# Six modulation vectors of a DiT-like network summed on TensorE instead of VectorE

## The chip, the cores and the metric

One NeuronCore of one Trainium2 chip runs the whole network as one program. The metric is the device time of one execution in microseconds (us); lower is better. TensorE (PE) multiplies, VectorE (DVE) and ScalarE (ACT) work on rows and evacuate results, SyncE (SP) issues nearly all loads.

## The reference, cut to what matters

An fp32 network over 256 tokens of width 1024: two layers of a mixer and a feed-forward part (the second of these a mixture of eight experts, two for each token), then two layers of attention and a feed-forward part. Each of the eight sublayers is modulated by a scale, a shift and a gate, which come from one conditioning vector c and a weight matrix:

```python
def modulation(c, w, b):
    m = jnp.einsum("bd,de->be", jax.nn.silu(c), w) + b
    shift, scale, gate = jnp.split(m, 3, axis=-1)
    return shift[:, None], scale[:, None], gate[:, None]
```

So there are 24 modulation vectors of 1024 numbers, each the product of silu(c) with a matrix of 1024x1024, that is of 4 MB of weights. The sublayer's input is xn * (1 + scale) + shift, its result is multiplied by the gate and added to x.

## The kernel before

The program goes through stages 1 to 8 (mixer, FFN, mixer, experts, attention, FFN, attention, FFN). Stage 4 has two parts: the route (norm, router, choice of experts, expert input) and the experts. Weights come in chunks of 1 MB (128 partitions x 2048) into the pool raw, are split by ScalarE (L159) and VectorE (L160) into a rounded part hi and a rest lo, and each product takes three matmuls (mm3, L178 to L180). Matmuls of plain fp32 go through mm (L183) and leave two records each in the trace; transposes go through tr (L187).

The modulation vectors are computed ahead of their use, named by (layer, sub, scale/shift/gate) with layers and subs from 0. A stage's plan lists those that it makes, and calls of fill spread their steps over the stage; one step is one chunk of 1 MB. There are two ways:

- mod_rows keeps a running sum macc of 128x1024 on VectorE: for each of eight rows of 128 weights macc += w * c (L318 for the first, L320 for the others), with c one number for each partition. At the end TensorE sums over the partitions: for a gate two matmuls with a matrix of ones, 128x512; for a scale or shift (in stages other than 2 and 6) eight matmuls that take 128 columns of macc as the weight and one column of ones, and L353 adds the bias.
- mod_gate_pe, before for the gate (0,0) alone, lets TensorE do the whole sum: sixteen matmuls of 128x512 that take c, spread over 128 columns, as the weight and the chunk as the moving side, and two with the bias.

The order on each engine is set by a scheduler that builds the program: code emitted earlier has priority, and fill is put back by LAG; within one engine the instructions then run strictly in the order given. SP is such a queue too: a load that waits for its buffer holds back all loads behind it. The pool raw has four buffers.

```python
        LAG = {1: 100, 3: 100, 4: 30, 5: 30}
        FILL = {1: (4, 1, 1, 3, 1, 2), 2: (3, 2, 2), 3: (1, 1, 1, 1, 0, 0), 6: (2, 3), 8: (1, 0)}
```

Names used below: raw is a loaded chunk, h a stage's modulated input, x and xn the residual stream and its norm, P attention probabilities, ysum the sum of the experts' results; pp, pa, pj, sa, sb, sd are pools of TensorE's results. L1071 to L1113 choose the experts, L1152 and behind it builds the experts' input.

Of the kernel before, what the change touches and what calls it, by code (L numbers as in the profile page):

```python
# [15 lines left out]
ALU = mybir.AluOpType  # L16
# [3 lines left out]
D = 1024  # L20
KD = 8
# [46 lines left out]
class _Net:  # L68
# [186 lines left out]
    def fill(self, n):  # L255

        with self.behind(), self.tc.high_priority(offset=-self.lag) if self.lag else nullcontext():
            for _ in range(n):
                if not self.modq:
                    return  # L260
                key = self.modq[0]
                if key in self.gates_pe:
                    self.mod_gate_pe(key)
                else:
                    self.mod_rows(key)
                self.modpos += 2
                if self.modpos == KD:
                    self.modpos = 0
                    self.modq.pop(0)
                    self.mods[key] = self.mod_done(key)  # L270
# [8 lines left out]
    def mod_gate_pe(self, key):  # L279

        nc = self.nc
        w, b, j, c0 = self.mod_src(key)
        if self.modpos == 0:
            self.modacc = self.tl("gate", [128, D])
            nc.gpsimd.dma_start(out=self.modacc[0:1, :], in_=b[j * D:(j + 1) * D].unsqueeze(0))
        g = self.modacc
        h, k0 = self.modpos // 4, self.modpos % 4 * 2
        hs = slice(h * 512, (h + 1) * 512)
        if k0 == 0:
            self.modps = self.ps(pool="pa")  # L290
            self.mm(self.modps, self.ones[0:1, :], g[0:1, hs], True, False)
        wv = w.rearrange("(k p) n -> p k n", p=128)
        v = self.raw(wv[:, k0:k0 + 4, j * D + h * 512:j * D + (h + 1) * 512])
        for i in range(4):
            c = self.csil[:, c0 + k0 + i:c0 + k0 + i + 1]
            self.mm(self.modps, c.to_broadcast([128, 128]), v[:, i], False, k0 + i == KD - 1)
        if k0 == 4:
            self.plus(key, g[:, hs], self.modps)

    def mod_rows(self, key):  # L300

# [19 lines left out]

    def mod_done(self, key):

        if key in self.gates_pe:
            return self.modacc
        l, s, name = key
        j, acc = self.mod_src(key)[2], self.modacc
        if name == "gate":
            g = self.tl("gate", [128, D])
            for h in range(2):  # L330
                hs = slice(h * 512, (h + 1) * 512)
                p = self.ps(pool=self.mps)
                self.mm(p, self.ones, acc[:, hs])
                self.plus(key, g[:, hs], p)
            return g
        c = self.tl("col", [128, KD])
        if self.step in (2, 6):

            sums = self.sc([128, KD])
            for k in range(0, KD, 4):  # L340
                p = self.ps((128, 4, 128), pool=self.mps)
                for q in range(4):
                    self.tr(p[:, q], acc[:, (k + q) * 128:(k + q + 1) * 128])
                for q in range(4):
                    self.nc.scalar.activation(p[:, q], p[:, q], ACT.Copy, accum_out=sums[:, k + q:k + q + 1])
        else:
            p = self.ps(pool=self.mps)
            for k in range(KD):
                self.mm(p[:, k:k + 1], acc[:, k * 128:(k + 1) * 128], self.ones[:, 0:1])
            sums = p[:, 0:KD]  # L350
        q = ((l * 2 + s) * 3 + j) * KD if l < 2 else ((l - 2) * 6 + j) * KD
        bc = (self.col3 if l < 2 else self.col4)[:, q:q + KD]
        self.nc.vector.scalar_tensor_tensor(c, sums, 1.0 if name == "scale" else 0.0, bc, ALU.add, ALU.add)  # L353
        return c
# [1146 lines left out]
    def run(self):  # L1501
        a, nc = self.a, self.nc
        FFN = dict(f=2, s2=10, sh=12, pp=4, pa=4)
        MIX = dict(sh=3, s1=2, w=4, g=3, kvl=1, cx=2, ct=4, cv=6, dc=3, cb=2, ys=2, ml=3, P=3, pj=2, sd=3, pa=3)
        ROUTE = dict(sh=4, s1=2, s2=4)
        MOE = dict(pp=2, ya=2, pa=4)
        EXP = dict(xe=1, s1=4, s2=6, s4=2, rawx=2)
        ATT = dict(sh=5, s1=2, qk=2, sq=3, v=2, qkT=6, on=3, P=5, y=6, pp=2, pj=2, sa=2, sb=2)
        SIZES = {1: MIX, 2: FFN, 3: MIX, 4: MOE, 5: ATT, 6: dict(FFN, f=4), 7: ATT, 8: FFN}

        SC, SH, GA = "scale", "shift", "gate"
        plan = {
            0: [(0, 0, SC), (0, 0, SH)],
            1: [(0, 0, GA), (0, 1, SC), (0, 1, SH)],
            2: [(0, 1, GA), (1, 0, SC), (1, 0, SH), (1, 0, GA), (1, 1, SC), (1, 1, SH)],
            3: [(1, 1, GA)],
            4: [(2, 0, SC), (2, 0, SH), (2, 0, GA)],
            5: [(2, 1, SC), (2, 1, SH)],
            6: [(2, 1, GA), (3, 0, SC), (3, 0, SH), (3, 0, GA), (3, 1, SC), (3, 1, SH)],
            8: [(3, 1, GA)],  # L1520
        }
        self.gates_pe = {(0, 0, GA)}
        LAG = {1: 100, 3: 100, 4: 30, 5: 30}
        FILL = {1: (4, 1, 1, 3, 1, 2), 2: (3, 2, 2), 3: (1, 1, 1, 1, 0, 0), 6: (2, 3), 8: (1, 0)}
        self.mods, self.modq, self.modpos = {}, [], 0
        with self.phase(sh=12, s1=1, s2=3, pp=4, pa=4):
            setup = self.setup()
            next(setup)
            self.mod_start(plan[0])
            x = self.load_x(a["x"])  # L1530
            xn = x = self.layer_norm(x)
            self.fill(KD * KD)
            for _ in setup:
                pass
            g, b = self.c1("ln0_g", 0), self.c1("ln0_b", 0)
            self.later = [lambda x=x: self.affine(x, a["ln0_g"], a["ln0_b"])]
        for s in range(1, 9):
            l, i = (s - 1) // 2, (s - 1) % 2
            self.step = s
            one = s < 5  # L1540
            if s == 2:
                self.later.append(self.rope_setup)
            with self.phase(**SIZES[s]):
                if one:
                    A, B = self.ab(l, i, g, b)
                else:
                    A, B = self.ab(l, i, self.c1("norm_ffn_2" if i else "norm_mix_2", l - 2))
                if s == 4:
                    self.bar = None
                    with self.phase(**ROUTE):  # L1550
                        self.mod_start(plan[4], LAG[4])
                        self.fill(KD * KD)
                        hf = self.make_hf(xn, A, B)
                        st = self.route(xn, hf)
                    with self.phase(**EXP):
                        order = self.granules()
                        ready = [self.raw(src) for src in order[:5]]
                        ready = [self.split(v) for v in ready[:2]] + ready[2:] + [self.raw(order[5])]
                        self.moe_over(st, A, B)
                        ysum = st[4]  # L1560
                        self.experts(0, *st[:4], A, B, ysum, order, True, ready)
                    get = lambda t, hh: ysum[t][hh]
                else:
                    h = self.make_h(xn, A, B)
                    self.mod_start(plan.get(s, []), LAG.get(s, 0))
                    if i == 0:
                        get = self.mixer(l, h, FILL[s]) if one else self.attn2(l - 2, h)
                    elif one:
                        get = self.ffn(h, a["ffn_w1"][0], a["ffn_w3"][0], a["ffn_w2"][0], FILL[s])
                    else:  # L1570
                        get = self.ffn(h, a["w_gate_2"][l - 2], a["w_up_2"][l - 2], a["w_down_2"][l - 2], FILL[s])
                rows = (a["post_ln_g"][l, i], a["post_ln_b"][l, i]) if one else None
                if s == 4:
                    x, xn = self.resid_rms(get, x, self.mod(l, i, "gate"), self.two_rows(*rows))
                else:
                    x, xn = self.resid(get, x, self.mod(l, i, "gate"), one, s < 8)
                if s < 4:
                    g, b = self.c1("post_ln_g", s - 1), self.c1("post_ln_b", s - 1)
                    x = xn
                    self.later.append(lambda x=x, r=rows: self.affine(x, *r))  # L1580
# [35 lines left out]
```

## Time and profile before

| | before |
|---|---|
| median of 3 runs (lowest to highest) | 2068.33 us (2067.39 to 2068.36) |
| profiled execution: its time, its span | 2068.1 us, 2066.0 us |
| TensorE busy | 1926.2 us, 93% |
| VectorE busy | 1643.8 us, 80% |
| ScalarE busy | 1208.2 us, 58% |
| mean granted clock of TensorE | 0.972 of full speed |

The span is the profiled part of one execution, and the time of that execution is 2.1 us longer. Busy time of TensorE counts matmuls; it can be busy at two clocks, 1.2 and 2.4 GHz, which the profile gives as granted clocks of 0.50 and 1.00.

### The profile page before, as it was taken

What the parts mean: (1) busy time and instruction counts of PE and PEld (TensorE: products, weight loads), DVE (VectorE), ACT (ScalarE), POOL (GpSimd) and SP (SyncE); (2) the same over time, 40 slices, a digit from 0 to 9 for tenths busy, and PEclk for the clock granted to TensorE, in tenths of its full rate; (3) what the DMA queues carried; (4) which work ended last, traced back from release to release, by engine and by line L of the source; (5) the groups of instructions that cost most, each with busy time, mean ns of one, the idle gap of its engine ahead of it and who ended that gap; (6) DMA issues with size and microseconds to landing.
All of it is one profiled execution on the core that took longest, in us unless ns stands there. A gap on an engine that the chain in (4) does not pass through costs nothing.

```text
span 2066.0 us, 29939 instructions
## 1 busy us (share of the span) xinstructions
PE 1926.2 (93%) x11481; PEld 1660.4 (80%) x11481; DVE 1643.8 (80%) x2412; ACT 1208.2 (58%) x1817; POOL 50.2 (2%) x100
## 2 busy tenths in 40 slices
PE   3998999898499999999999999969989999998999
PEld 3887999886378787878778888858869998978998
DVE  6888987898598888888888888889778887667554
ACT  3455445562488767767776777755554546555442
POOL 4000000100000000000000000000000000000000
PEclk9999999998699999999999999979999999999999
DMA  9576999665399999899999999958339995326662
GB/s 325 184 276 214 348 329 316 195 223 205 144 330 362 339 332 341 319 357 346 345 326 350 348 355 358 364 187 279 138 119 349 335 328 164 123 86 220 204 204 82
DMA packets 283238, 555.25 MB, mean 269 GB/s; under 512 B 10172, under 2 KB 137520, under 8 KB 283088
## 3 DMA queue, kind: packets, MB, share of 16 engines
q1 hardware_dynamic: 280000, 549.49, 75.1%
q0 software_dynamic: 2656, 3.20, 0.9%
q8 instruction: 91, 1.49, 0.3%
q10 hardware_dynamic: 432, 0.58, 0.1%
q14 instruction: 59, 0.48, 0.1%
HBM read 552.19 MB, written 1.05 MB: 268 GB/s over the span
## 4 chain that ended last, share of the span: by engine, by line
PE 63%; DVE 6%; ACT 2%; issue 2%; DMA 0%; ACTq 0%; DVEq 0%
PE pp L179 11%; PE pp L180 11%; PE pp L178 11%; PE pa L654 6%; PE ya L179 4%; PE ya L178 4%; PE ya L180 4%; PE pp L187 3%; DVE lo L160 2%; PE pj L178 2%; PE pj L179 1%; PE pj L180 1%; PE sa L183 1%; PE pp L183 1%; ACT hi L159 1%
## 5 line engine op out<-in xcount | busy, mean ns | idle before, releaser
L160 DVE TENSOR_TENSOR lo<-raw,hi 128x1024 fp32r<-128x1024 f32 x660 | 786.0, 1219 | 177.3 <-ACT hi L159 168.6
L159 ACT CAST hi<-raw 128x1024 fp32r<-128x1024 f32 x660 | 667.4, 1050 | 344.2 <-PE pp L179 141.8
L178 PE MATMUL pp<-h,hi 128*128 128x256 f32 x960 | 270.7, 282 | 0.0
L180 PE MATMUL pp<-h,lo 128*128 128x256 f32 x960 | 267.8, 279 | 0.0
L179 PE MATMUL pp<-h,hi 128*128 128x256 f32 x960 | 267.7, 279 | 0.0
L160 DVE TENSOR_TENSOR lo<-rawx,hi 128x1024 fp32r<-128x1024 f32 x176 | 208.3, 1219 | 40.2 <-ACT hi L159 38.9
L320 DVE SCALAR_TENSOR_TENSOR macc<-raw,const,macc 128x1024 f32<-128x1024 f32 x168 | 215.2, 1281 | 9.9 <-DMA raw<-in_w_mod_dram 7.1
L180 PEld LDWEIGHTS pp<-h,lo 128*128 128x128 f32 x960 | 182.2, 190 | 0.1
L159 ACT CAST hi<-rawx 128x1024 fp32r<-128x1024 f32 x176 | 176.9, 1050 | 9.2 <-PE pp L180 7.4
L179 PEld LDWEIGHTS pp<-h,hi 128*128 128x128 f32 x960 | 180.6, 188 | 1.7 <-issue 1.2
L178 PEld LDWEIGHTS pp<-h,hi 128*128 128x128 f32 x960 | 180.3, 188 | 1.7 <-ACT hi L159 1.0
L179 PE MATMUL pp<-lo,h 128*128 128x512 f32 (+1 forms) x480 | 174.9, 365 | 1.3 <-DVE lo L160 1.0
L178 PE MATMUL pj<-hi,h 128*128 128x256 f32 x576 | 168.3, 293 | 7.2 <-ACT h L530 4.0
L178 PE MATMUL pp<-hi,h 128*128 128x512 f32 (+1 forms) x480 | 173.5, 362 | 0.2 <-ACT f L528 0.2
L179 PE MATMUL pj<-lo,h 128*128 128x256 f32 x576 | 165.1, 288 | 1.8 <-DVE lo L160 1.8
L180 PE MATMUL pj<-hi,h 128*128 128x256 f32 x576 | 164.8, 288 | 0.0
L654 PE MATMUL pa<-hi,s 128*128 128x512 f32 x528 | 148.2, 390 | 0.0
L179 PE MATMUL pp<-lo,xe 128*128 128x512 f32 (+1 forms) x384 | 144.9, 377 | 1.2 <-DVE lo L160 1.0
L180 PE MATMUL pp<-hi,x 128*128 128x512 f32 (+1 forms) x384 | 143.7, 374 | 0.0
L178 PE MATMUL pp<-hi,xe 128*128 128x512 f32 (+1 forms) x384 | 143.6, 374 | 0.0
L180 PE MATMUL pp<-hi,xe 128*128 128x512 f32 (+1 forms) x384 | 143.1, 373 | 0.0
L179 PE MATMUL ya<-lo,s 128*128 128x512 f32 x352 | 140.8, 400 | 0.0
(474 smaller groups left out, 3518.5 us busy)
## 6 DMA issues: line engine op xcount, KB each, us to landing
raw<-in_moe_w_dram SPq DMA_DIRECT2D x176, 1024.0 KB, 6.3
rawx<-in_moe_w_dram SPq DMA_DIRECT2D x88, 1024.0 KB, 6.3
raw<-in_ada_w_dram SPq DMA_DIRECT2D x48, 1024.0 KB, 6.7
raw<-in_w_mod_dram SPq DMA_DIRECT2D x48, 1024.0 KB, 6.9
raw<-in_w_in_dram SPq DMA_DIRECT2D x42, 1024.0 KB, 6.0
raw<-in_ffn_w_dram SPq DMA_DIRECT2D x33, 1024.0 KB, 6.3
raw<-in_w_gate_dram SPq DMA_DIRECT2D x22, 1024.0 KB, 5.2
raw<-in_w_up_dram SPq DMA_DIRECT2D x22, 1024.0 KB, 5.3
```

The costliest lines, as they stand in the source:

```text
L159: self.nc.scalar.copy(h, v[:, z:z + m])
L160: self.nc.vector.tensor_tensor(l, v[:, z:z + m], h.bitcast(F32), ALU.subtract)
L178: mm(out, lhsT=a[0], rhs=b[0], start=start, stop=False)
L179: mm(out, lhsT=a[0], rhs=b[1], start=False, stop=False)
L180: mm(out, lhsT=a[1], rhs=b[0], start=False, stop=stop)
L183: self.nc.tensor.matmul(out, lhsT=lhsT, rhs=rhs, start=start, stop=stop)
L187: self.nc.tensor.transpose(out, in_, self.ident[:p, :p])
L320: V.scalar_tensor_tensor(acc, v[:, i], c, acc, ALU.mult, ALU.add)
L654: mm(accs[t][h], lhsT=y[ia][:, s], rhs=W[ib][:, h * 512:(h + 1) * 512], start=start and ia == 0 and ib == 0, stop=stop and ia == 1)
```

## The change

Two more gates are made by mod_gate_pe: (1,1) in stage 3, and (2,0), which moves from the plan of the route into a call of fill behind the experts, with results in the pool pp. Four column vectors are made by a new function, mod_cols_pe: the shift (0,1) in stage 1, the scale and shift (2,0) in the route, the shift (2,1) in stage 5. It takes 128x128 of a chunk as the weight and one column of c as the moving side, two matmuls for each 128 columns and chunk, thus 16 a chunk and 64 a vector; VectorE adds the 128x8 results of the four chunks and the bias.

```diff
@@ fill
                 if key in self.gates_pe:
                     self.mod_gate_pe(key)
+                elif key in self.cols_pe:
+                    self.mod_cols_pe(key)
                 else:
                     self.mod_rows(key)
@@ mod_gate_pe
         if k0 == 0:
-            self.modps = self.ps(pool="pa")
+            self.modps = self.ps(pool=self.gps)
@@
+    def mod_cols_pe(self, key):
+        V = self.nc.vector
+        w, b, j, c0 = self.mod_src(key)
+        if self.modpos == 0:
+            self.modacc = self.tl("col", [128, KD])
+        wv = w.rearrange("(k p) n -> p k n", p=128)
+        v = self.raw(wv[:, self.modpos:self.modpos + 2, j * D:(j + 1) * D])
+        p = self.ps(pool=self.mps)
+        for q in range(KD):
+            for i in range(2):
+                k = c0 + self.modpos + i
+                self.mm(p[:, q:q + 1], v[:, i, q * 128:(q + 1) * 128], self.csil[:, k:k + 1], i == 0, i == 1)
+        if self.modpos == 0:
+            V.scalar_tensor_tensor(self.modacc, p[:, 0:KD], 1.0 if key[2] == "scale" else 0.0, self.mod_bias(key), ALU.add, ALU.add)
+        else:
+            V.tensor_tensor(self.modacc, self.modacc, p[:, 0:KD], ALU.add)
@@ mod_done
-        if key in self.gates_pe:
+        if key in self.gates_pe or key in self.cols_pe:
             return self.modacc
@@ run
-            4: [(2, 0, SC), (2, 0, SH), (2, 0, GA)],
+            4: [(2, 0, SC), (2, 0, SH)],
...
-        self.gates_pe = {(0, 0, GA)}
+        self.gates_pe = {(0, 0, GA), (1, 1, GA), (2, 0, GA)}
+        self.gps = "pa"
+        self.cols_pe = {(0, 1, SH), (2, 0, SC), (2, 0, SH), (2, 1, SH)}
@@ run, stage 4, behind the experts
                     get = lambda t, hh: ysum[t][hh]
+                    self.gps = "pp"
+                    self.mod_start([(2, 0, GA)])
+                    self.fill(KD)
+                    self.gps = "pa"
```

What stands on TensorE in the route, from the last matmul of stage 3's output projection (L654 before, L680 now) to the router (128x8, L183). Before:

```order
L654 MATMUL pa_5189<-hi_5274,h_4720 128x512
L183 MATMUL pp_5437<-const_115,macc_5419 128x1 x8
L183 MATMUL pp_5465<-const_115,macc_5447 128x1 x8
...
L183 MATMUL pp_5495<-macc_5475,const_115 128x512
L183 MATMUL pp_5498<-macc_5475,const_115 128x512
L187 MATMUL pp_5502<-const_113,x_5327 128x128 x4
L187 MATMUL pp_5509<-const_113,x_5327 128x128 x4
L187 MATMUL pp_5516<-const_113,x_5327 128x128 x4
L187 MATMUL pp_5523<-const_113,x_5327 128x128 x4
L183 MATMUL pp_5532<-sh_5530,h_5501 128x8 x16
```

The left-out rows are four short matmuls that start ysum. In the changed kernel, with the same four left out behind the first two rows of one column:

```order
L183 MATMUL pp_5481<-const_121,raw_5479 128x1 x16
L183 MATMUL pp_5501<-const_121,raw_5499 128x1 x16
...
L183 MATMUL pp_5521<-const_121,raw_5519 128x1 x16
L183 MATMUL pp_5541<-const_121,raw_5539 128x1 x16
L183 MATMUL pp_5562<-const_121,raw_5560 128x1 x16
L183 MATMUL pp_5582<-const_121,raw_5580 128x1 x16
L183 MATMUL pp_5602<-const_121,raw_5600 128x1 x16
L183 MATMUL pp_5622<-const_121,raw_5620 128x1
L187 MATMUL pp_5641<-const_113,x_5386 128x128 x4
L183 MATMUL pp_5622<-const_121,raw_5620 128x1 x15
L187 MATMUL pp_5648<-const_113,x_5386 128x128 x4
```

Sixteen one-column matmuls and two of the gate stood ahead of the transposes of xn; now 113 one-column matmuls stand ahead of the first four transposes and 15 more ahead of the other twelve.

What stands on TensorE in stage 1 where the last projection (pj, L178 to L180) ends and the output projection begins (L676 and L680 now). In the changed kernel the 27 rows of one column further up alternate with the projection like the first rows here:

```order
L183 MATMUL pa_1402<-const_121,raw_1400 128x1
L179 MATMUL pj_1498<-lo_1495,h_343 128x256
L183 MATMUL pa_1402<-const_121,raw_1400 128x1
L180 MATMUL pj_1498<-hi_1494,h_344 128x256
L183 MATMUL pa_1402<-const_121,raw_1400 128x1 x5
L183 MATMUL pa_1559<-const_121,raw_1557 128x1 x16
L183 MATMUL pa_1579<-const_121,raw_1577 128x1 x16
L676 MATMUL pj_1635<-raw_1639,ml_1083 128x512
```

Before, the output projection (L650) followed on the projection's last row, and eight one-column matmuls alternated with its own.

What stands on TensorE behind the last expert (ya is the last expert's result, pa the four ysum results, sa and L187 belong to stage 5). In the changed kernel:

```order
L180 MATMUL ya_16001<-hi_16824,s_16793 128x512
L183 MATMUL pp_16861<-raw_16863,const_121 128x512
L183 MATMUL pa_5719<-s_16840,s_14834 128x512
...
L183 MATMUL pa_5722<-s_16841,s_14834 128x512
L183 MATMUL pp_16861<-raw_16863,const_121 128x512 x3
L183 MATMUL pp_16861<-raw_16869,const_121 128x512 x4
L183 MATMUL pp_16876<-gate_16859,const_115 128x512
L183 MATMUL pp_16876<-raw_16878,const_121 128x512 x4
L183 MATMUL pp_16876<-raw_16884,const_121 128x512 x4
```

Before, the four ysum results were followed by the first rows of stage 5 at once. SP issues the four chunks of this gate directly behind the experts' last loads, and behind them the rows post_ln_g and post_ln_b of stage 4's norm, which wait for TensorE to be done with the first chunk, and the first five loads of w_in for stage 5.

## Rows read from the trace of the kernel before

**Rows 1.** The page's first part: busy us, share of the span, instructions.

```profile
PE 1926.2 (93%) x11481; PEld 1660.4 (80%) x11481; DVE 1643.8 (80%) x2412; ACT 1208.2 (58%) x1817; POOL 50.2 (2%) x100
```

**Rows 2.** Stretches: length, busy us (count) of PE, PEld, DVE, ACT, POOL; clock, DMA, GB/s.

```profile
80.00:120.00 40.00, 39.98 (x205) 26.46 (x205) 30.09 (x64) 19.46 (x51) 0.31 (x1) 1.00 0.61 210
150.00:175.00 25.00, 25.00 (x112) 18.64 (x111) 17.84 (x44) 8.32 (x15) 0.00 (x0) 1.00 0.61 208
440.00:470.00 30.00, 26.34 (x169) 22.09 (x169) 25.61 (x56) 13.16 (x34) 0.00 (x0) 0.94 0.49 180
470.00:490.00 20.00, 14.56 (x57) 10.78 (x57) 13.98 (x47) 7.36 (x24) 0.90 (x1) 0.66 0.44 153
1363.00:1385.00 22.00, 4.96 (x19) 3.10 (x19) 19.68 (x45) 10.09 (x14) 0.00 (x0) 0.61 0.27 92
1385.00:1392.00 7.00, 6.26 (x30) 5.69 (x29) 7.00 (x24) 7.00 (x19) 0.00 (x0) 0.52 0.67 203
1420.00:1460.00 40.00, 38.52 (x305) 35.02 (x304) 36.98 (x88) 20.32 (x40) 0.00 (x0) 1.00 0.76 264
```

**Rows 3.** TensorE's timeline: start us, us, line, op, out<-in, form, records.

```profile
22.49 3.55 PE L183 MATMUL pp<-const,macc 128*128 128x1 f32 x16 [2.80 <-DVE macc L320]
...
79.30 4.56 PE L183 MATMUL pa<-raw,const 128*128 128x512 f32 x10
...
512.82 3.62 PE L183 MATMUL pp<-const,macc 128*128 128x1 f32 x32
```

**Rows 4.** VectorE's instructions on macc: ns min/median/max, first and last start.

```profile
L320 DVE SCALAR_TENSOR_TENSOR macc<-raw,const,macc x168: 1271/1283/1289, 12.0 to 1969.5; 128x1024 f32<-128x1024 f32 x168
L318 DVE TENSOR_SCALAR macc<-raw,const x16: 743/748/818, 11.2 to 1673.6; 128x1024 f32<-128x1024 f32 x16
```

**Rows 5.** Short stretches of the route, columns as in rows 2.

```profile
513.00:516.30 3.30, 3.30 (x31) 3.30 (x32) 3.09 (x9) 0.00 (x0) 1.28 (x2) 1.00 0.00 0
516.30:520.00 3.70, 1.03 (x6) 0.30 (x5) 3.60 (x11) 0.00 (x0) 0.19 (x1) 0.71 0.01 1
...
535.00:540.00 5.00, 2.78 (x20) 1.92 (x18) 4.10 (x7) 2.64 (x5) 0.00 (x0) 1.00 1.04 392
540.00:545.00 5.00, 4.84 (x31) 4.75 (x30) 0.22 (x2) 0.00 (x0) 0.00 (x0) 0.68 0.81 313
545.00:550.00 5.00, 2.27 (x10) 2.21 (x10) 2.58 (x17) 0.21 (x1) 0.00 (x0) 0.50 0.00 0
```

**Rows 6.** TensorE's timeline of the route; in brackets idle us before and what ended it.

```profile
516.31 1.02 PE L183 MATMUL pa<-const 128*128 128x512 bf16 x4
531.72 3.55 PE L183 MATMUL pp<-macc,const 128*128 128x512 f32 x4 [14.39 <-DVE macc L320]
535.11 0.60 PE L187 MATMUL pp<-const,x 128*128 128x128 f32 x4
...
539.70 5.15 PE L183 MATMUL pp<-sh,h 128*128 128x8 f32 x32 [0.78 <-DVE h L508]
546.91 2.27 PE L183 MATMUL pp<-t,const 128*128 128x8 f32 x10 [2.06 <-DVE t L1086]
554.99 0.55 PE L183 MATMUL pp<-s,x 128*128 128x256 f32 x1 [5.82 <-DVE s L1152]
```

**Rows 7.** TensorE's waits in 440 to 490: us in total, times, longest.

```profile
PE pa L187 <- DVE P L943: 6.7, 2, 4.2
```

**Rows 8.** Timelines of SP, TensorE and VectorE behind the experts.

```profile
1346.79 0.34 SPq L479 DMA_DIRECT2D raw<-in_post_ln_g_dram  x1
...
1363.35 2.24 PE L183 MATMUL pa<-s,s 128*128 128x512 f32 x8 [0.33 <-ACT s L1261]
...
1372.19 1.27 DVE L608 SCALAR_TENSOR_TENSOR x<-x,t,raw 128x1024 f32<-128x1024 f32 x1
...
1383.73 1.97 PE L187 MATMUL pp<-const,x 128*128 128x128 f32 x8 [12.37 <-DVE x L615]
1386.45 1.11 PE L187 MATMUL pp<-const,x 128*128 128x128 f32 x4 [0.74 <-ACT sq L528]
```

More of the change, by code (lines that the diff above doesn't have):

```diff
@@ L298, in mod_gate_pe, with mod_bias @@
             self.plus(key, g[:, hs], self.modps)
+    def mod_cols_pe(self, key):
[14 more added lines that the diff above has]
+            V.tensor_tensor(self.modacc, self.modacc, p[:, 0:KD], ALU.add)
+    def mod_bias(self, key):
+        l, s, name = key
+        j = self.mod_src(key)[2]
+        q = ((l * 2 + s) * 3 + j) * KD if l < 2 else ((l - 2) * 6 + j) * KD
+        return (self.col3 if l < 2 else self.col4)[:, q:q + KD]
     def mod_rows(self, key):
```

## The prediction

> **What bounds the kernel now.** I read four views. The page's first part shows TensorE busy for 93% of the span and VectorE for 80% [rows 1]. That mean hides different stages, so the second view is the table of busy time by stretch: TensorE has no idle time in stage 1 (39.98 of 40 us, 25.00 of 25), and nearly none in stage 5 (38.52 of 40, with VectorE at 36.98). It has idle time around the attention of stage 3 (14.56 of 20) and in the gap behind the experts (4.96 of 22) [rows 2]. The third view, TensorE's timeline of the route, shows an engine that stands still for 14.39 us until VectorE has summed the last modulation vector [rows 6]. The fourth, the granted clock in short stretches of that route, matters most here [rows 5]. So VectorE's sums cost time in the route and in stage 3; in stages 1 and 5 each microsecond given to TensorE is one more to wait for.
>
> **What one vector costs.** On VectorE a vector takes eight passes of 1.283 us, the first of a column vector 0.748 [rows 4]: 9.7 us or, for a gate, 10.3. Six vectors free 59 us of VectorE. A column vector becomes 64 one-column matmuls with a 128x128 weight, in place of eight of the same form. The trace has this form: 512.82 shows 32 records, two to a matmul, in 3.62 us, or 3.62/16 = 0.226 us a matmul under a full clock; 22.49 shows 16 records in 3.55, 0.44 a matmul and twice as long [rows 3]. I take the second for the price under the lower clock, because the route's ten 8-column records take 2.27 us under 0.50, 0.45 a matmul [rows 5, 6]. The sums use 0.226 and 0.43 (the last record's tail taken off). Per vector that is 56 more matmuls, 12.7 us at the full clock. A gate becomes 16 matmuls of 128x512 plus two for the bias: 79.30 shows ten records in 4.56, so 0.9 with the tail and about 0.86 without it [rows 3]. Less the two it had, that is 16 x 0.86 = 13.8 us more TensorE.
>
> The Trainium skill would price the first form otherwise: its page "TensorE: Matmul & The Clock Gate", section "Back-to-back issue gap", gives 1 to 64 columns about 60 cycles or a floor near 25 ns, so 0.05 us a matmul. By that a vector would cost 3 us. The rows give four times as much, and I go by them.
>
> **The clock.** At 512.82 the clock is full. TensorE then runs 16 one-column matmuls and four short ones, is busy for 3.30 of 3.30 us, and yet the granted clock reads 0.71 in 516.3 to 520 [rows 5]; the one-column run had begun 3.5 us before that stretch. The router is plainer. Its 32 records of 8 columns start at 539.70 [rows 6]; TensorE is busy for 4.84 of the 5 us from 540, and the clock of that stretch is 0.68, behind 1.00 before it and ahead of 0.50 after it [rows 5]. So a TensorE that is without a pause on such narrow matmuls has lost its clock in this trace. 0.71 over 3.7 us means that the fall came 1.6 us in, at 517.9, or 5 us after the narrow run began.
>
> The Trainium skill says that the clock follows how busy TensorE has been (same page, "What's actually happening"). If the busy time of the profile were that, long runs of one-column matmuls would stay at the full clock; the router's row differs. This is a rival below.
>
> **The change, stage by stage.** Times are against the profiled execution.
>
> *Stage 1, the shift of (0,1).* In the order of the changed kernel 27 of the 64 matmuls alternate with the last projection, and 37 stand together ahead of the output projection. TensorE has no wait there that could hide them: +12.7. 37 together are 8.4 us at the full clock. If it falls after 5 us, as in the route, 15 of them cost 0.2 more each, 3.1, and the projection behind them starts at the lower clock. I take +4 for the clock between 0 and 9: **+16.5** (11 to 22).
>
> *Stage 3, the gate of (1,1).* +13.8 on TensorE. Against it: 5.4 us idle and a clock of 0.66 in 470 to 490, and 3.7 us idle before it [rows 2]. The order now puts some hundred projection matmuls and half the gate into these waits, and takes VectorE's passes out of the softmax chain, for which TensorE waits 6.7 us [rows 7]. 9 us of idle time filled, 5 back from the half-speed work of 470 to 490 (a clock of 0.66 is 0.68 of the time at one half; 0.68 of 14.56 is 9.9, which the full clock halves), and two passes of 1.28 less on the chain: 16.7. **-3** (-8 to +4).
>
> *Stage 4, the route.* Here the order decides. Let T be 512.8, the end of the output projection. Before, 16 one-column matmuls, then the gate's wait, the first transposes at 535.11 (T+22.3), the router at 539.70 (T+26.9), expert input at 554.99 (T+42.2) [rows 3, 6]. After, 113 one-column matmuls stand ahead of the first four transposes and 15 more ahead of the other twelve; TensorE takes its queue in order, so xn waits for them whether or not it is ready. 128 at the full clock are 28.9 us. With the clock as in the row: 5.0 us at 0.226 are 22 matmuls, and 106 are left at 0.43: 45.6. The four ysum starts take 1.0 at 516.31 [rows 6], so 2.0; sixteen transposes at 1.11 for four, as under the 0.52 of 1385 to 1392 [rows 2, 8], 4.4; the step to the router 0.8 [rows 6]. Sum 57.8, against 26.9: +30.9. The router at 0.43 takes 6.9 in place of 5.15, +1.7. Six weight splits on VectorE now stand among the router's small steps; nearly all can run while the matmuls do, +0.5 (0 to 4). The relief of VectorE (the 14.39 us wait is gone) is already in these sums, as TensorE's queue is now the later. **+33** (+7 to +38).
>
> *Behind the experts, the gate of (2,0).* 13.7 us of matmuls in a hole of 18.1 (1365.6 to 1383.73) [rows 8]: covered. What it pushes: SP now issues the four gate loads ahead of the post_ln rows, and these take the buffer of the first gate chunk. They had been issued at 1346.79, long before VectorE's L608 at 1372.19 needs them [rows 8]; now they wait until TensorE is through with that chunk, about 1369, and land after a megabyte's flight. VectorE's queue stands at L608 meanwhile, with the norm and the transposes behind it: +1.5, and two gate copies in ScalarE's part of the chain +1.5; further w_in loads wait likewise, +1; the clock at 1385 may be kept, -1. **+3** (0 to +8). If the hole were not there, 13.7.
>
> *Stage 5, the shift of (2,1).* +12.7 in a stage with 1.5 us idle in 40 [rows 2]. VectorE, at 36.98 of 40, loses 9.7, of which I let 4 shorten TensorE's waits (0 to 9.7): +7. The 64 stand in runs of 16, two and two close together, 7 to 8 us each with little wide work among them: for the clock +4 (0 to 8). **+11** (+2 to +18).
>
> FFNs and experts keep their order: 0. Sum: 16.5 - 3 + 33 + 3 + 11 = +60.5. The profiled execution took 2068.1 us (span 2066.0 and 2.1 around it), 0.2 below the median: **2129 us**.
>
> **Rivals.** *The clock holds.* If one-column runs don't cost the clock, the route is 28.9 + 1.0 + 2.4 + 0.8 = T+33.1, with a router at full speed +5 to +7, and stages 1 and 5 lose their 4 each: +26, 2094. For it: sixteen at 513 to 516.3 ran at 1.00 throughout [rows 5]. Against it: the router. 0.17.
> *Cheap matmuls: faster.* If weight loads of stationary chunks that come straight from a load hide each other, a matmul at 0.05 makes stage 1 +2.8 and the route's 128 only 6.4, less than the norm takes; then VectorE's chain, without the passes that TensorE awaited for 14.39 us, sets the transposes some 8 earlier: -8, stage 3 -5, gap +1, stage 5 -2: -11, 2057. Zero is crossed near 0.1 a matmul, less than half of the row [rows 3]. 0.04, and 0.03 for no change.
> *Slots and splits as well.* The forecast, with the gap at +8, the splits at +4 and stage 5 at +18: 2145. 0.08.
> *Forecast.* 0.68.
>
> **How the numbers follow.** The forecast's own range is 2110 to 2146 by the bounds above. To leave out no more than 2 in 10 the range takes in the rival of the full clock: 2090 to 2146. A measurement here tells 0.2% (4 us) from no change. Faster 0.04, within 0.2% 0.03, slower 0.93.
>
> **What would show it.** Right: the route from the last output projection to the expert input grows from 42 to about 75 us, the one-column matmuls there step at 0.43, the granted clock reads 0.50 from some 5 us in; 37 together in stage 1; the hole behind the experts filled and L608 some us late. Wrong: a clock of 1.00 through the one-column runs, or steps far below 0.2 us; a stage 3 that gives back more than 10.

## The result and the profile after

The changed kernel takes 2158.8 us (median of 4 runs, 2157.9 to 2159.8) against 2068.4 for the kernel before, measured beside it: a ratio of 1.043 (95% interval 1.042 to 1.0446), or 90 us more. The forecast was 2129 with a range of 2090 to 2146: the sign and most mechanisms held, and the size was too small.

The first two parts of the page of the changed kernel (busy us with shares, and the granted clock in 40 slices):

```profile
PE 2053.0 (95%) x11993; PEld 1771.0 (82%) x11993; DVE 1595.8 (74%) x2376; ACT 1211.4 (56%) x1819; POOL 48.6 (2%) x98
...
PEclk9997999999569999999999999999889999999999
```

Against [rows 1] TensorE is busy for 127 us more and VectorE for 48 us less. Forecast were 78 us more of TensorE at the full clock (56 x 0.226 for four vectors, 13.8 for two gates); most of the other part of the 127 is work that ran at the lower clock. The clock line dips in the slices of stage 1 (7 tenths), of stage 4's route (5 and 6) and of stage 5 (8 and 8).

Where the 92 us of span went is read from the starts of the same instructions in both traces: the first transposes of the next stage's input, the last matmul of the output projection of stage 3, the first expert input, the last ysum matmul.

| stretch | before, us | change, us | forecast |
|---|---|---|---|
| stage 1 and before | 178.7 | +29.3 | +16.5 |
| stage 2 (FFN) | 201.7 | +0.2 | 0 |
| stage 3 | 132.2 | -2.0 | -3 |
| route | 42.4 | +35.8 | +33 |
| experts | 810.2 | +2.7 | 0 |
| gap behind the experts | 18.5 | +0.4 | +3 |
| stage 5 | 145.3 | +26.0 | +11 |
| stages 6 to 8 | 537.0 | -0.4 | 0 |

The table of short stretches of the changed kernel, columns as in [rows 2] (the third number from the right, behind the five engines, is the granted clock):

```profile
148.00:152.00 4.00, 4.00 (x38) 4.00 (x37) 1.38 (x2) 0.00 (x0) 0.00 (x0) 1.00 0.00 0
152.00:156.00 4.00, 4.00 (x22) 4.00 (x21) 0.32 (x3) 0.00 (x0) 0.00 (x0) 0.51 0.00 0
160.00:165.00 5.00, 5.00 (x25) 5.00 (x25) 0.16 (x1) 1.18 (x2) 0.00 (x0) 0.50 0.00 0
175.00:180.00 5.00, 5.00 (x18) 3.97 (x19) 1.12 (x6) 1.30 (x5) 0.00 (x0) 0.50 0.22 57
180.00:185.00 5.00, 5.00 (x16) 2.50 (x15) 4.36 (x15) 1.99 (x4) 0.00 (x0) 0.72 0.47 192
499.60:519.60 20.00, 19.41 (x113) 14.76 (x112) 9.21 (x14) 7.88 (x13) 0.00 (x0) 1.00 0.57 208
540.00:545.00 5.00, 5.00 (x44) 4.92 (x43) 2.93 (x11) 0.00 (x0) 0.53 (x1) 0.96 0.00 1
545.00:560.00 15.00, 15.00 (x68) 14.08 (x69) 1.83 (x7) 0.00 (x0) 0.00 (x0) 0.50 0.44 146
560.00:580.00 20.00, 20.00 (x95) 20.00 (x95) 3.76 (x11) 3.14 (x2) 0.00 (x0) 0.50 0.45 153
1449.00:1456.00 7.00, 5.10 (x23) 4.60 (x24) 7.00 (x27) 6.37 (x15) 0.00 (x0) 0.51 1.03 328
1520.00:1524.00 4.00, 4.00 (x39) 4.00 (x37) 2.12 (x8) 2.19 (x8) 0.00 (x0) 1.00 0.00 0
1524.00:1530.00 6.00, 6.00 (x32) 6.00 (x31) 0.31 (x3) 1.10 (x4) 0.00 (x0) 0.52 0.12 29
1562.00:1570.00 8.00, 8.00 (x35) 7.33 (x36) 0.95 (x4) 1.09 (x4) 0.00 (x0) 0.50 0.48 169
```

In each of the three stages that got column vectors there are stretches in which TensorE is busy without a pause and its clock is at one half. In stage 1 the fall is at 152, in the run where one-column matmuls alternate with the projection, and it lasts to about 182.8. TensorE's timeline of the changed kernel shows what it costs (start, us, form, records, two to a matmul):

```profile
151.65 0.28 PE L183 MATMUL pa<-const,raw 128*128 128x1 f32 x2
...
153.57 0.42 PE L183 MATMUL pa<-const,raw 128*128 128x1 f32 x2
153.85 0.56 PE L180 MATMUL pj<-hi,h 128*128 128x256 f32 x1
...
162.32 15.78 PE L183 MATMUL pa<-const,raw 128*128 128x1 f32 x74
177.96 5.23 PE L676 MATMUL pj<-raw,ml 128*128 128x512 f32 x6
...
540.36 9.74 PE L183 MATMUL pp<-const,raw 128*128 128x1 f32 x64
549.96 1.87 PE L183 MATMUL pa<-const 128*128 128x512 bf16 x4
551.62 34.56 PE L183 MATMUL pp<-const,raw 128*128 128x1 f32 x162
586.04 1.09 PE L187 MATMUL pp<-const,x 128*128 128x128 f32 x4
...
596.84 6.94 PE L183 MATMUL pp<-sh,h 128*128 128x8 f32 x32
...
618.28 0.55 PE L183 MATMUL pp<-s,x 128*128 128x256 f32 x1 [7.05 <-DVE s L1178]
```

The 37 that stand together take 15.78/37 = 0.427 us each, not 0.226; the 81 of the route 34.56/81 = 0.427 as well. Expert input starts 78.1 us after the last matmul of the output projection, against 42.4 [rows 6].

### The profile page after: what moved, and what is told of

Its sections match the earlier page's. It is cut to its first block, busy times and chain, and to the rows that moved or that the text cites. A ratio compares the mean times of both kernels' runs of the same rounds, so it can differ in the third digit from the quotient of the medians.

```text
span 2157.9 us, 30945 instructions
## 1 busy us (share of the span) xinstructions
PE 2053.0 (95%) x11993; PEld 1771.0 (82%) x11993; DVE 1595.8 (74%) x2376; ACT 1211.4 (56%) x1819; POOL 48.6 (2%) x98
## 4 chain that ended last, share of the span: by engine, by line
PE 61%; DVE 6%; ACT 3%; issue 2%; DVEq 0%; ACTq 0%
PE pp L179 11%; PE pp L180 10%; PE pp L178 10%; PE pa L680 5%; PE ya L179 4%; PE ya L178 3%; PE ya L180 3%; DVE lo L160 2%; PE pp L183 2%; PE pp L187 2%; PE pj L179 1%; PE pj L178 1%; PE pj L180 1%; PE sa L183 1%; PE sb L183 1%
## 5 line engine op out<-in xcount | busy, mean ns | idle before, releaser
L178 PE MATMUL pp<-h,hi 128*128 128x256 f32 x960 | 270.7, 282 | 0.0
L180 PE MATMUL pp<-h,lo 128*128 128x256 f32 x960 | 267.7, 279 | 0.0
L180 PEld LDWEIGHTS pp<-h,lo 128*128 128x128 f32 x960 | 182.1, 190 | 0.0
L178 PEld LDWEIGHTS pp<-h,hi 128*128 128x128 f32 x960 | 180.4, 188 | 1.7 <-ACT hi L159 1.0
L178 PE MATMUL pj<-hi,h 128*128 128x256 f32 x576 | 170.9, 298 | 5.8 <-ACT h L556 4.1
L178 PE MATMUL pp<-hi,h 128*128 128x512 f32 (+1 forms) x480 | 173.3, 362 | 0.2 <-ACT f L554 0.2
L180 PE MATMUL pj<-hi,h 128*128 128x256 f32 x576 | 168.2, 294 | 0.0
L346 DVE SCALAR_TENSOR_TENSOR macc<-raw,const,macc 128x1024 f32<-128x1024 f32 x124 | 159.0, 1282 | 9.8 <-DMA raw<-in_w_mod_dram 6.6
L680 PE MATMUL pa<-hi,s 128*128 128x512 f32 x528 | 148.2, 390 | 0.0
L180 PE MATMUL pp<-hi,x 128*128 128x512 f32 (+1 forms) x384 | 143.5, 374 | 0.0
L178 PE MATMUL pp<-hi,xe 128*128 128x512 f32 (+1 forms) x384 | 143.5, 374 | 0.0
L180 PE MATMUL pp<-hi,xe 128*128 128x512 f32 (+1 forms) x384 | 143.0, 372 | 0.0
```

Source lines behind the costliest of these rows:

```text
L178: mm(out, lhsT=a[0], rhs=b[0], start=start, stop=False)
L180: mm(out, lhsT=a[1], rhs=b[0], start=False, stop=stop)
L346: V.scalar_tensor_tensor(acc, v[:, i], c, acc, ALU.mult, ALU.add)
L680: mm(accs[t][h], lhsT=y[ia][:, s], rhs=W[ib][:, h * 512:(h + 1) * 512], start=start and ia == 0 and ib == 0, stop=stop and ia == 1)
```

## Experiments

Times are medians, against the median of the kernel before measured beside them. All of them are the changed kernel with the edit shown. The changes by stretch, in us, from the same starts as above (the kernel before has a span of 2066.0):

| run | stage 1 | stage 3 | route | experts | gap | stage 5 | profiled span |
|---|---|---|---|---|---|---|---|
| gates only | -0.6 | +6.2 | -2.8 | +2.9 | +0.4 | +3.4 | 2075.4 |
| 64 columns | +13.6 | -1.9 | +11.2 | +4.1 | +0.3 | +17.8 | 2110.0 |
| shift (0,1) alone | +28.9 | +0.5 | -0.3 | +1.5 | 0.0 | -1.3 | 2094.4 |
| shift (2,1) alone | -1.0 | +0.9 | +0.3 | +0.3 | 0.0 | +26.8 | 2092.5 |
| gate behind the experts alone | -0.8 | -0.4 | -4.5 | +1.7 | +0.4 | -1.0 | 2061.1 |
| gate of stage 3 alone | 0.0 | +6.0 | +2.4 | +2.8 | +0.1 | -2.9 | 2073.6 |
| gate behind, route's columns | -1.1 | -1.4 | +36.6 | +2.5 | +0.3 | -1.6 | 2101.7 |
| gate behind, splits behind | -0.5 | -0.4 | -7.6 | +4.1 | +0.3 | -0.1 | 2062.3 |
| gate behind, splits at the router | -1.0 | -0.7 | -8.5 | +4.5 | +0.3 | +0.3 | 2060.3 |

Stages that an edit doesn't touch move by up to 3 us in a single profile (stage 5 above all), so entries below that say little.

### The gates without the column vectors

```diff
-        self.cols_pe = {(0, 1, SH), (2, 0, SC), (2, 0, SH), (2, 1, SH)}
+        self.cols_pe = set()
```

> The four column vectors are summed on VectorE again, the two gates stay on TensorE. If the one-column matmuls with the clock that they cost are the whole loss, stages 1 and 5 and the experts return to the times of before, stage 3 keeps its -2, the gap its +0.4, and the route loses the wait for the gate (the first transposes at T+12 in place of T+22): about 2056 us (2050 to 2066). If the gates are part of the loss (slots of the load buffers, the post_ln rows behind them), it stays above 2068, up to 2080.

Measured: 2077.3 us against 2067.8, ratio 1.0044 (1.0027 to 1.0061). Stage 1 and the gap came back as expected. The experts and stage 5 did not come back whole (+2.9 and +3.4), the route gave back 2.8 instead of 10 or more, and stage 3 lost 6.2. So the second case holds, in stage 3 by the first of the causes that it named, the load buffers, and in the route by one that it did not name. What SP waited for in 400 to 485, then VectorE's timeline of this run in stage 3 and the route:

```profile
SPq L131 <- PE pa L183: 20.9, 4, 10.3
```

```profile
485.14 0.75 DVE L344 TENSOR_SCALAR macc<-raw,const 128x1024 f32<-128x1024 f32 x1 [4.79 <-DMA raw<-in_w_mod_dram]
...
503.24 1.14 DVE L1038 TENSOR_SCALAR ys<-ys,t 128x256 f32<-128x256 f32 x4
...
525.53 1.17 DVE L160 TENSOR_TENSOR lo<-raw,hi 128x1024 fp32r<-128x1024 f32 x1
526.68 1.21 DVE L160 TENSOR_TENSOR lo<-raw,hi 128x1024 fp32r<-128x1024 f32 x1
527.88 1.21 DVE L160 TENSOR_TENSOR lo<-raw,hi 128x1024 fp32r<-128x1024 f32 x1
529.14 1.22 DVE L160 TENSOR_TENSOR lo<-raw,hi 128x1024 fp32r<-128x1024 f32 x1
530.34 1.22 DVE L160 TENSOR_TENSOR lo<-raw,hi 128x1024 fp32r<-128x1024 f32 x1
```

SP waits 20.9 us for matmuls of the gate (pa, L183) to give their buffers free, a wait that the kernel before does not have, and issues the first chunk of the route's first vector at 479.71, where the kernel before issues it at 440.57. VectorE waits for that chunk until 485.14; its passes then stand between the small steps of the norm that scales ys (L1038), and TensorE waits 4.6 us for that. In the route six splits of expert weights, 1.2 us each, stand in the norm of x: one from 522.16 and the five above. The time that the passes freed was filled with other work by the scheduler, which cannot know that this norm is being waited for.

### The same matmuls with 64 columns

```diff
-                self.mm(p[:, q:q + 1], v[:, i, q * 128:(q + 1) * 128], self.csil[:, k:k + 1], i == 0, i == 1)
+                self.mm(p[:, q * 64:(q + 1) * 64], v[:, i, q * 128:(q + 1) * 128],
+                        self.csil[:, k:k + 1].to_broadcast([128, 64]), i == 0, i == 1)
+        p = p.rearrange("p (q n) -> p q n", n=64)[:, :, 0]
```

> The changed kernel, with the one column of c spread to 64 columns, so that each of the same 256 matmuls streams 64 equal columns; the order in the route stays (113 matmuls ahead of the first transposes), in stages 1 and 5 the scheduler spreads them a little more. If the clock is what the one-column runs cost beside their own 0.226 us, it stays at 1.00 and the time falls although each matmul does more: stage 1 +13, route +7, stage 5 +9 against the kernel before, about 2096 us (2090 to 2110). If the number of matmuls, their weight loads or their place set the time, it stays at 2159 or rises. If the clock falls in spite of 64 columns, 2159 as well, and the granted clock shows it.

Measured: 2110.6 us, ratio 1.0198 (1.0168 to 1.0229): 48 us less than the changed kernel with 64 times the columns. The timeline of the route in this run, and then short stretches of stages 1, 4 and 5:

```profile
535.78 14.46 PE L183 MATMUL pp<-const,raw 128*128 128x64 f32 x128
550.27 0.66 PE L187 MATMUL pp<-const,x 128*128 128x128 f32 x4
```

```profile
140.00:160.00 20.00, 20.00 (x179) 20.00 (x177) 5.44 (x15) 3.01 (x8) 0.00 (x0) 1.00 0.24 79
...
540.00:550.00 10.00, 10.00 (x92) 10.00 (x91) 0.40 (x3) 0.00 (x0) 0.00 (x0) 1.00 0.90 283
...
558.00:570.00 12.00, 5.89 (x31) 5.82 (x30) 6.78 (x14) 4.80 (x6) 0.00 (x0) 0.51 0.59 205
...
1521.00:1531.00 10.00, 10.00 (x34) 7.78 (x35) 4.52 (x17) 3.77 (x16) 0.00 (x0) 0.50 0.60 182
```

64 matmuls take 14.46 us, 0.226 each, the price of one column at the full clock, and the clock stays at 1.00 until 558, 1 us into the router's matmuls of 8 columns. Place, number and weights are those of the changed kernel in the route, but for a few neighbours that change places; what differs is the streamed columns. So in the route it is the one-column form that costs the clock, and not the number of matmuls, their weight loads or their place. Stage 1 keeps the clock too, and there the same alternation with the projection runs from 148 to 157; behind it the order differs, with 19 of the matmuls in a row where the changed kernel has 37. The time is just above the range of 2090 to 2110. Two sizes were off: the route has +11 in place of +7, and stage 5 has +18 in place of +9; there the last of the matmuls, alternating with short score matmuls, still lost the clock (1521 to 1531): half of these 10 us is 5, and 12.7 + 5 is the 18.

### Each column vector by itself

```diff
-        self.cols_pe = {(0, 1, SH), (2, 0, SC), (2, 0, SH), (2, 1, SH)}
+        self.cols_pe = {(0, 1, SH)}
```

and the gates and the plan of stage 4 as before; for the second run {(2, 1, SH)} in its place.

> The kernel before with the shift (0,1) alone as one-column matmuls in stage 1. If the clock's fall in the mixed stretch and behind it is the cause, the whole +29 of that stage comes back: 2097 us (2093 to 2100), clock at 0.50 for about 30 us. If only the added 56 matmuls count and the rest came from the other parts of the change, +13: 2081 us.

> The kernel before with the shift (2,1) alone as one-column matmuls in stage 5. If the two falls of the clock there are the cause, +26: 2094 us (2088 to 2098), two stretches of some 17 us at 0.50. If the stage was late because of the gate behind the experts (loads of w_in later), only +9: 2077 us.

Measured: 2096.1 us, ratio 1.0139 (1.0122 to 1.0157), for the first, 2095.1 us, ratio 1.0136 (1.0119 to 1.0153), for the second. Each stage's loss comes back whole without the rest of the change: +28.9 in stage 1, +26.8 in stage 5. The short stretches of the first run:

```profile
140.00:151.00 11.00, 11.00 (x99) 11.00 (x97) 3.00 (x6) 1.62 (x5) 0.00 (x0) 1.00 0.08 30
151.00:160.00 9.00, 9.00 (x44) 9.00 (x43) 0.32 (x3) 0.00 (x0) 0.00 (x0) 0.50 0.32 117
160.00:178.00 18.00, 18.00 (x87) 18.00 (x86) 1.52 (x4) 1.18 (x2) 0.00 (x0) 0.50 0.33 117
```

and of the second:

```profile
1461.00:1475.00 14.00, 14.00 (x68) 14.00 (x68) 0.47 (x4) 1.93 (x6) 0.00 (x0) 0.51 0.35 112
1475.00:1498.00 23.00, 22.94 (x192) 21.90 (x190) 15.51 (x43) 11.86 (x20) 0.00 (x0) 1.00 0.47 161
1498.00:1516.00 18.00, 18.00 (x74) 15.21 (x74) 6.57 (x24) 4.22 (x13) 0.00 (x0) 0.53 0.35 117
```

Some 31 us at one half of the clock in either, with TensorE busy for all of it: half of that, 15 us, is what the full clock would have saved. 12.7 + 15 is 28, against 28.9 and 26.8.

### Each gate by itself

```diff
-        self.gates_pe = {(0, 0, GA), (1, 1, GA), (2, 0, GA)}
+        self.gates_pe = {(0, 0, GA), (2, 0, GA)}
```

without column vectors; for the second run {(0, 0, GA), (1, 1, GA)} with the plan of stage 4 as before.

> The kernel before with one edit: the gate (2,0) is made by TensorE behind the experts, and no longer by VectorE in the route. In the run with both gates the hole behind the experts was filled at +0.4 us, yet the experts ended 1 to 2 us later against their start and stage 5 took 3.4 us more, and the route gave back 2.8. If the late loads of w_in behind the four gate chunks are the cause of the 3.4: stage 5 +3.4 here too, sum about +3: 2071 us (2067 to 2074). If these belonged to the other gate, the route's gain stands alone: 2064 us.

> The kernel before with the gate (1,1) alone on TensorE in stage 3; the column vectors and the gate (2,0) stay on VectorE in the route. In the run with both gates stage 3 took 6.2 us more, though in the changed kernel it took 2.0 less. If its chunks hold the load buffers, so that the passes for the route's vectors come later and stand in the norm ahead of the output projection: stage 3 +5 to +9 and the route 0 to +4: 2078 us (2073 to 2083). If the +6.2 was chance of that one schedule, or the gate helps: 2066 us.

Measured: the gate behind the experts 2065.8 us against 2069.7, ratio 0.9984 (0.9972 to 0.9995), a gain at the edge of the noise; the gate of stage 3 2080.2 us, ratio 1.0062 (1.0045 to 1.0079). The first was expected to repeat the +3.4 of stage 5 and did not (-1.0): w_in's loads are not its cause, or not each time, and it stays open. The second repeats the loss of stage 3, +6.0, with the same wait for ys in TensorE's table of waits (the other row is the route's norm) and the same 20.9 us in SP's:

```profile
PE pp L183 <- DVE t L607: 10.8, 1, 10.8
PE sd L187 <- DVE ys L1038: 4.6, 1, 4.6
```

So this gate is a loss as long as VectorE sums the route's column vectors, and the -2.0 of the changed kernel in stage 3 needs those to have left VectorE. What the gate itself then gives is not shown: the next run, in which the route's column vectors leave VectorE and this gate stays on it, has -1.4 in stage 3.

### The route's columns on top of the gate behind

```diff
-        self.cols_pe = set()
+        self.cols_pe = {(2, 0, SC), (2, 0, SH)}
```

> The kernel of the gate behind the experts, and beside it the two column vectors of (2,0) as one-column matmuls in the route: the difference to that kernel is what 128 one-column matmuls cost there. By the clock (half speed from some 5 us on, as the changed kernel's trace shows) the route takes about 36 us more than before; stage 3 gains 2 to 4 since its passes leave: about 2103 us (2098 to 2110). By 0.226 us a matmul alone: 2080 us.

Measured: 2103.7 us, ratio 1.018 (1.0159 to 1.0201), near the 2103 expected with the clock's fall and far from the 2080 without it: the route goes from -4.5 to +36.6, 41 us for 128 matmuls, in place of 16, that take 28.9 at the full clock, although TensorE's idle time ahead of the router, 11.6 us in the run with the gate behind alone, now holds a part of them. The clock fell 2.2 us after the first of them (510.39 to 512.6), and not 5.

### The splits out of the way

```diff
-                        ready = [self.split(v) for v in ready[:2]] + ready[2:] + [self.raw(order[5])]
+                        with self.tc.issue_after(self.last.ins), self.tc.high_priority(offset=-60):
+                            ready = [self.split_now(v) for v in ready[:2]] + ready[2:]
+                        ready = ready + [self.raw(order[5])]
```

on the kernel of the gate behind the experts.

> The kernel of the gate behind the experts, with the six weight splits that VectorE does among the route's norm and router steps tied behind the route's last step. With both gates on TensorE the route gave back only 2.8 of the 14.4 us that TensorE had waited for the gate, because six splits of 1.2 us took the place of the passes in the norm. If that is the cause, the expert input starts 7 to 10 us earlier after the output projection, and the first expert then waits 2 to 4 us for its splits: about 5 us below the kernel of the gate behind the experts, 2065 us. If the norm waits for something else, the same time as that kernel, or more by the splits now in front of the first expert.

Measured: 2063.6 us against 2069.7, ratio 0.9969 (0.9959 to 0.998). VectorE's timeline of this run:

```profile
518.44 0.16 DVE L607 SCALAR_TENSOR_TENSOR t<-t,t 128x1 f32<-128x1 f32 x1
...
534.02 0.17 DVE L1097 COPY t<-pp 128x16 f32<-128x16 f32 x1 [6.23 <-PE pp L183]
...
543.04 3.50 DVE L160 TENSOR_TENSOR lo<-raw,hi 128x1024 fp32r<-128x1024 f32 x3 [3.02 <-DVEq L1149]
```

The norm's last step is at 518.44, and at 524.00 in the run with the gate behind alone, where five splits stood in it. The four splits of the two chunks tied now stand among the last steps ahead of L1178 and take back 3 of these 5.6 us; the experts take 2.4 more. The idea was right, its size less than expected.

The last run moves four of them into the 6.23 us for which VectorE waits for the router.

```diff
...
-        V.tensor_copy(L, p[:, 0:16].rearrange("p (t e) -> p t e", t=2))
+        with self.tc.issue_after(self.seen.ins):
+            mid()
+        with self.tc.issue_after(self.cut.ins):
+            V.tensor_copy(L, p[:, 0:16].rearrange("p (t e) -> p t e", t=2))
...
```

In the lines left out mid splits the first two chunks, seen is the last step of the route's modulated input, and cut is the last split.

> The kernel of the gate behind the experts, with the first four weight splits tied between the route's modulated input and the copy of the router's result, where VectorE stood idle for 6.2 us in the run with the splits behind the route. If that idle time holds them, the route keeps the -8 of that run (two further splits stay among the router's small steps, +2) and the first expert has its splits ready (+4 back to +1.5): 2061 us against 2069 for the kernel before (2058 to 2065). If the splits' loads or ScalarE's casts are late there, the copy of the router's result waits for them: 2066 us or more.

Measured: 2064.4 us against 2069.1, ratio 0.9985 (0.9974 to 0.9995): the splits fit where they were put, the route is 8.5 us shorter than before, and the experts still take 4.5 more, so nothing is gained over the run before it. The first expert's matmuls start 10.6 us behind the expert input, 9.5 in the kernel before: the expert input runs at one half of the clock for 8.3 us here, 3.8 before. Where the rest of the 4.5 comes from isn't settled, but for the gate's bias, which stands among the last expert's matmuls for 1.1 us. Both kernels are faster than the one before, by 0.3% and 0.15%, and than the changed one; both keep all of the column vectors on VectorE.

## Why the prediction was wrong in its size

*What failed.* The term "+4 for the clock" of stage 1, and its twin in stage 5. The prediction counted 15 matmuls at the lower clock, of the 37 that stand together, and the start of the work behind them. The trace has the fall 4 us into the mixed run (27 matmuls between rows of the projection, which I had let pass as wide work) and half speed for 30.7 us. So 52 of the 64 ran at the lower clock, 15 of them in the mixed run and the 37 behind it at 0.427 each, and the projection's rows and the first output rows between and behind them ran at half speed as well. Sized by the run with 64 columns, which keeps the clock there, the term is 29.3 - 13.6 = 15.7 us, not 4, beyond its bound of 9. In stage 5 the column vector alone costs 26.8 where +7 were counted, with +4 for the clock. The +7 is 12.7 less 5.7: 4 of relief are named, and the other 1.7 are not explained (the 1.5 us of idle time stand beside them). Here half speed for about 31 us is 15, and of the relief about 1 us arrived (12.7 + 15 against 26.8). Both stages lie above their own bounds, 29.3 above 22 and 26.0 above 18, and together they are off by 28 us, nearly all of the 30.

*The clock as such.* Right: it falls, though TensorE is without a pause. In the route 4.2 us after the first one-column matmul (5 were forecast, from 512.8 in [rows 3, 5]) and to the price forecast, 0.43 a matmul. That the 5 us came so near is luck: the row they were read from has TensorE idle from 517.3 on (516.31 and 1.02 in [rows 6]), 0.6 us ahead of the fall at 517.9, and in the run with the route's columns the fall came after 2.2 us. "TensorE: Matmul & The Clock Gate" of the Trainium skill ("What's actually happening") has the clock follow how busy TensorE has been; by the busy time of the profile the route would have kept 1.00 for 40 us, and it shows 0.50 with 20.00 of 20.00 us busy. The rival *the clock holds* is out, and the run with 64 columns shows about what it would have given: 2111 with 10 us of stage 5 still at one half, where 2094 was its sum.

*The route.* +33 forecast, +35.8 measured, by the steps forecast: first transposes at 45.7 us behind the projection's end (586.04 less 540.36; 46 by the same sum), the router at 56.5 in place of 57.8 and 6.94 us long (6.9). The rest is 14.5 us from the router's end to the expert input, 10.1 before: four splits of 1.22 us on VectorE among the small steps between 604.4 and 610.0, priced at +0.5 with a bound of 4, where the difference is 4.4.

*Stage 3.* -3 forecast, -2.0 measured. The waits were filled as told: in 499.6 to 519.6, the stretch as far behind the stage's start as 470 to 490 was before, TensorE is busy for 19.41 of 20 us at 1.00, where [rows 2] had 14.56 at 0.66. The runs add a condition that the prediction lacked: the gain is there only because the column passes left VectorE too, and without this gate that alone gave -1.4. So the nearness to -3 does not show that the gate was priced right.

*Behind the experts.* +3 forecast, +0.4 measured. The order of the loads was as told, but no step waited for it. The loads and the norm's step that needs the rows, of the changed kernel:

```profile
1434.16 0.34 SPq L505 DMA_DIRECT2D raw<-in_post_ln_g_dram  x1
```

```profile
1438.21 1.28 DVE L634 SCALAR_TENSOR_TENSOR x<-x,t,raw 128x1024 f32<-128x1024 f32 x1
```

The last ysum matmul starts at 1431.17, so this step comes 7.0 us behind it, just as before (1372.19 in [rows 8], behind 1365.19). The rows landed in time. The 1 us counted for the clock did not come: it fell once more at 1449.2, just ahead of the transposes at 1450.09, and reads 0.51 in 1449 to 1456.

*The experts.* +2.7 against 0. About 1.1 each lie at their two ends: the expert input runs at one half of the clock until 626.5, 8.2 us behind its start (3.8 us before), and one of the gate's matmuls, its bias at 1422.46, stands among the last expert's. Between them the first and the last-but-one block keep their distance to 0.3 us.

*Cheap matmuls.* Out. The Trainium skill's floor near 25 ns ("Back-to-back issue gap") does not bear on a run that loads a new 128x128 weight for each column: 0.113 us a record at the full clock and 0.213 at the lower one, here.

## What to carry to other kernels

In these runs a matmul of one column with a new 128x128 weight cost as much as one of 64 columns, and a run of them cost the clock: count all work that stands in the run and behind it at half speed, and don't count a run as broken by the wide rows in between until a trace shows that it is. TensorE's busy share says nothing of this; the granted clock beside it does. When an engine is relieved in a chain that others wait for, look at what the scheduler puts in the freed time: here splits took the place of the sums, and only tying them behind the chain let a part of the gain through.

## What was not expected of the hardware

The 64 columns of the second experiment cost nothing: 0.226 us a matmul with one column and with 64, at the full clock, so here more streamed work made the kernel 48 us faster. And the weight load followed the clock. In the one-column runs of the route PEld is busy throughout (20.00 of 20.00 us in 560 to 580), its records last 192 ns at a granted clock of 1.00 and 333 ns at 0.50, and the matmuls went from 0.226 to 0.427 us, though they stream next to nothing.
